# Loading row pairs as 64 KB runs into three slots shared by x and y, in a kernel that takes row-wise cosine similarities

## The chip, the cores and the metric

The kernel runs on one core of one Trainium2 chip. The time is device microseconds (us) of one execution. "Last data" below is the end of the last load packet in the trace's packet records, and "tail" is what follows it until the span ends. A DMA engine is called dry, or idle, when it has no packet under way, and its next packet after that is a restart.

## The reference

```python
x, y: float32 [8192, 8192]
out = sum(x * y, axis=1) / (norm(x, axis=1) * norm(y, axis=1) + 1e-8)
```

Every element of x and y is read once: 536.87 MB. Per row there are three sums: of x*x, y*y and x*y.

## The kernel before

A tile is 128 rows, one row of 32 KB on each partition. x and y have two buffers each. VectorE takes the dot (product and sum in one instruction); ScalarE takes the two sums of squares. SyncE issues the loads of tile t+2 as soon as tile t is free.

```python
xpool = tile_pool(name="xpool", bufs=2); ypool = tile_pool(name="ypool", bufs=2)
...
def issue_dma(t):                       # last tile: cut into 2 and 5 pieces
    nc.sync.dma_start(out=xtiles[t], in_=xv[t])      # 128 runs of 32 KB
    nc.sync.dma_start(out=ytiles[t], in_=yv[t])
...
def compute_tile(t):
    nc.vector.tensor_tensor_reduce(out=prod_s, in0=xt, in1=yt, ..., accum_out=xy_acc[:, t:t+1])  # prod_s bf16
    nc.scalar.activation(out=sq_s, in_=xt, func=Square, accum_out=xx_acc[:, t:t+1])
    nc.scalar.activation(out=sq_s, in_=yt, func=Square, accum_out=yy_acc[:, t:t+1])
...
# last tile: VectorE also squares the first 2048 columns of x, ScalarE the rest
```

Of the kernel before, what the change touches and what calls it, by code (L numbers as in the profile page):

```python
# [7 lines left out]


@with_exitstack  # L10
def kernel(
# [6 lines left out]
    nc = tc.nc  # L18
    P = nc.NUM_PARTITIONS

    n_rows, n_cols = x.shape
    assert n_rows % P == 0
    n_tiles = n_rows // P

    fp32 = mybir.dt.float32
    bf16 = mybir.dt.bfloat16

    xv = x.rearrange("(t p) k -> t p k", p=P)
    yv = y.rearrange("(t p) k -> t p k", p=P)

    xpool = ctx.enter_context(tc.tile_pool(name="xpool", bufs=2))
    ypool = ctx.enter_context(tc.tile_pool(name="ypool", bufs=2))
    sqpool = ctx.enter_context(tc.tile_pool(name="sqpool", bufs=1))
    prodpool = ctx.enter_context(tc.tile_pool(name="prodpool", bufs=1))
    accpool = ctx.enter_context(tc.tile_pool(name="accpool", bufs=1))
    finpool = ctx.enter_context(tc.tile_pool(name="finpool", bufs=1))
    psumpool = ctx.enter_context(tc.tile_pool(name="psum", bufs=1, space=bass.MemoryType.PSUM))

    xtiles = [
        xpool.tile([P, n_cols], fp32, tag="x", name=f"xt{t}")  # L40
        for t in range(n_tiles)
    ]
    ytiles = [
        ypool.tile([P, n_cols], fp32, tag="y", name=f"yt{t}")
        for t in range(n_tiles)
    ]

    last = n_tiles - 1

    HALF = n_cols // 2  # L50

    XCH = [(0, HALF), (HALF, n_cols)]
    Q = n_cols // 8
    YCH = [(0, 2 * Q), (2 * Q, 4 * Q), (4 * Q, 6 * Q), (6 * Q, 7 * Q), (7 * Q, n_cols)]

    def issue_dma(t):
        if t == last:
            for a, b in XCH:
                nc.sync.dma_start(out=xtiles[t][:, a:b], in_=xv[t, :, a:b])  # L59
            for a, b in YCH:  # L60
                nc.sync.dma_start(out=ytiles[t][:, a:b], in_=yv[t, :, a:b])  # L61
        else:
            nc.sync.dma_start(out=xtiles[t], in_=xv[t])  # L63
            nc.sync.dma_start(out=ytiles[t], in_=yv[t])  # L64

    issue_dma(0)
    issue_dma(1)

    dummy = finpool.tile([P, 1], fp32, tag="dummy")
    nc.scalar.memzero(dummy)  # L70
    nc.scalar.sqrt(out=dummy, in_=dummy)  # L71

    ident = finpool.tile([P, P], fp32, tag="ident")
    make_identity(nc, ident)

    xx_acc = accpool.tile([P, n_tiles], fp32, tag="xx")
    yy_acc = accpool.tile([P, n_tiles], fp32, tag="yy")
    xy_acc = accpool.tile([P, n_tiles], fp32, tag="xy")

    prod_s = prodpool.tile([P, n_cols], bf16, tag="prod")  # L80
    sq_s = sqpool.tile([P, n_cols], bf16, tag="sq")

    res = finpool.tile([P, n_tiles], fp32, tag="res")
    nn = finpool.tile([P, n_tiles], fp32, tag="nn")
    den = finpool.tile([P, n_tiles], fp32, tag="den")
    rcp = finpool.tile([P, n_tiles], fp32, tag="rcp")
    res_t_ps = psumpool.tile([n_tiles, P], fp32, tag="res_t_ps")
    res_t = finpool.tile([n_tiles, P], fp32, tag="res_t")
    res_t_ps_last = psumpool.tile([2, P], fp32, tag="res_t_ps_last")
    res_row_last = finpool.tile([2, P], fp32, tag="res_row_last")  # L90
    out_v = out.rearrange("(t p) -> t p", p=P)

    def compute_tile(t):
        xt = xtiles[t]
        yt = ytiles[t]
        nc.vector.tensor_tensor_reduce(  # L96
            out=prod_s,
            in0=xt,
            in1=yt,
            scale=1.0,  # L100
            scalar=0.0,
            op0=mybir.AluOpType.mult,
            op1=mybir.AluOpType.add,
            accum_out=xy_acc[:, t:t + 1],
        )
        nc.scalar.activation(  # L106
            out=sq_s,
            in_=xt,
            func=mybir.ActivationFunctionType.Square,
            accum_out=xx_acc[:, t:t + 1],  # L110
        )
        nc.scalar.activation(  # L112
            out=sq_s,
            in_=yt,
            func=mybir.ActivationFunctionType.Square,
            accum_out=yy_acc[:, t:t + 1],
        )

    def chain(cols, ps, sb, orows):
        nc.vector.tensor_tensor(  # L120
            out=nn[:, cols], in0=xx_acc[:, cols], in1=yy_acc[:, cols],
            op=mybir.AluOpType.mult,
        )
        nc.scalar.activation(  # L124
            out=den[:, cols], in_=nn[:, cols],
            func=mybir.ActivationFunctionType.Sqrt,
        )
        nc.vector.reciprocal(out=rcp[:, cols], in_=den[:, cols])  # L128
        nc.vector.tensor_tensor(  # L129
            out=res[:, cols], in0=xy_acc[:, cols], in1=rcp[:, cols],  # L130
            op=mybir.AluOpType.mult,
        )
        nc.tensor.transpose(out=ps, in_=res[:, cols], identity=ident)  # L133
        nc.vector.tensor_copy(out=sb, in_=ps)  # L134
        nc.sync.dma_start(out=out_v[orows, :], in_=sb)

    for t in range(n_tiles - 1):
        if t + 2 < n_tiles:
            issue_dma(t + 2)
# [114 lines left out]
```

## Time and profile before

| | before |
|---|---|
| time, median | 1256.36 us (1256.19 to 1256.38, 3 runs) |
| span of the profiled run | 1254.4 us |
| bytes read, mean rate | 536.87 MB, 428 GB/s |
| ScalarE busy, VectorE busy | 73%, 45% |
| last data, tail | 1248.1 us, 6.3 us |

The page's rows of 40 equal slices show how busy the DMA engines are (9 is 90% or more) and what they moved. All but the last slice are full. A packet is counted whole in the slice in which it starts, so the GB/s row scatters.

```profile
DMA  9999999999999999999999999999999999999997
GB/s 401 435 435 435 429 430 428 435 434 435 429 429 430 434 433 435 429 428 432 434 434 435 428 428 432 435 434 434 428 428 433 435 433 433 427 430 432 435 434 307
DMA packets 19227, 536.97 MB, mean 428 GB/s; under 512 B 2132, under 2 KB 2196, under 8 KB 2452
```

The Trainium skill, "DMA: Bandwidth & Descriptors", section "Where 436 GB/s comes from", gives a ceiling of 435.2 GB/s on the side of the core's on-chip memory. The best slices here show 435; with each packet spread over its length, the slices between the first and the last lie at 431 to 433. So the trace agrees within 1%. At that rate the bytes need 1233.6 us (an estimate: 536.87 MB over 435.2 GB/s).

The chain that ended last, by engine, says the same: three quarters of it is waiting for loads.

```profile
DMA 76%; DVE 22%; SPq 1%; issue 1%; DVEq 0%; PE 0%; ACT 0%
```

The costliest groups (columns: line, engine, operation, tiles, shapes, count | busy us, mean ns of one | idle us before them and what ended it) give the durations: 8.69 us for a dot over 8192 columns, 7.03 us for a square.

```profile
L96 DVE CUSTOM_DVE_ANT_0 prod_s<-xt,yt 128x8192 bf16<-128x8192 f32 x63 | 547.6, 8692 | 687.5 <-DMA yt<-in_y_dram 687.5
L106 ACT ACTIVATE sq_s<-xt 128x8192 bf16<-128x8192 f32 x63 | 442.9, 7031 | 168.5 <-DMA xt<-in_x_dram 168.5
```

The timeline of one tile (columns: start us, length us, engine, line, operation; the idle time before it and its releaser in brackets) shows the rhythm.

```profile
606.17 7.03 ACT L112 ACTIVATE sq_s<-yt 128x8192 bf16<-128x8192 f32 x1 [2.59 <-DMA yt<-in_y_dram]
606.25 8.69 DVE L96 CUSTOM_DVE_ANT_0 prod_s<-xt,yt 128x8192 bf16<-128x8192 f32 x1 [10.72 <-DMA yt<-in_y_dram]
...
615.01 0.33 SPq L63 DMA_DIRECT2D xt<-in_x_dram  x1
615.43 0.38 SPq L64 DMA_DIRECT2D yt<-in_y_dram  x1
...
626.01 8.69 DVE L96 CUSTOM_DVE_ANT_0 prod_s<-xt,yt 128x8192 bf16<-128x8192 f32 x1 [11.06 <-DMA yt<-in_y_dram]
```

y lands, the dot runs from 606.25, and 8.76 us later SyncE issues the next x and y. At that moment x of the next tile is about to land and its y, which lands at 626.0, is queued behind it, so the DMA engines still have about 11 us of work. What the issue waits for is the dot.

The issues (last column: us from issue to landing) show that loads wait in a queue: 9.7 us of transfer (8 packets of 1.21 us on each DMA engine) takes 20 to 30 us from issue to landing.

```profile
xt<-in_x_dram SPq DMA_DIRECT2D x63, 4096.0 KB, 20.2
yt<-in_y_dram SPq DMA_DIRECT2D x63, 4096.0 KB, 29.5
```

### The profile page before, as it was taken

The numbers are of one execution on the slowest core, as the hardware profiler recorded it, in microseconds if no ns is written. First come the engines' busy times: TensorE is split into PE (matmuls) and PEld (weight loads), VectorE is DVE, ScalarE is ACT, GpSimd is POOL, SyncE is SP. The second block draws the span as 40 slices with busy tenths as digits, with TensorE's granted clock in tenths as the row PEclk, the third lists the DMA queues.
The fourth block names the chain that finished last, engine by engine and source line by source line (L and its number), as shares of the span: only waits on it lengthen the run. The fifth ranks groups of instructions, "written<-read, shape, count | busy, mean of one in ns | idle before, by whom it ended". The sixth has DMA issues, their size and how long they took to land.

```text
span 1254.4 us, 933 instructions
## 1 busy us (share of the span) xinstructions
PE 0.8 (0%) x2; PEld 0.2 (0%) x2; DVE 561.6 (45%) x147; ACT 915.0 (73%) x276; POOL 0.7 (0%) x6
## 2 busy tenths in 40 slices
PE   0000000000000000000000000000000000000000
PEld 0000000000000000000000000000000000000000
DVE  2354353443534535445354353453544525445356
ACT  5777767776777767776777767776777767776777
POOL 0000000000000000000000000000000000000000
DMA  9999999999999999999999999999999999999997
GB/s 401 435 435 435 429 430 428 435 434 435 429 429 430 434 433 435 429 428 432 434 434 435 428 428 432 435 434 434 428 428 433 435 433 433 427 430 432 435 434 307
DMA packets 19227, 536.97 MB, mean 428 GB/s; under 512 B 2132, under 2 KB 2196, under 8 KB 2452
## 3 DMA queue, kind: packets, MB, share of 16 engines
q1 hardware_dynamic: 19220, 536.91, 99.5%
q14 instruction: 7, 0.06, 0.0%
HBM read 536.87 MB, written 0.03 MB: 428 GB/s over the span
## 4 chain that ended last, share of the span: by engine, by line
DMA 76%; DVE 22%; SPq 1%; issue 1%; DVEq 0%; PE 0%; ACT 0%
DMA yt<-in_y_dram 76%; DVE prod_s L96 21%; SPq L63 1%; DVE prod_s L186 0%; DVEq L96 0%; SPq L64 0%; SPq L61 0%; SPq L59 0%; DVE xy_acc L96 0%; PE res_t_ps_last L221 0%; DVE res_row_last L222 0%; ACT den L212 0%; DVE rcp L216 0%; DVE res L217 0%; DVE xy_acc L204 0%
## 5 line engine op out<-in xcount | busy, mean ns | idle before, releaser
L96 DVE CUSTOM_DVE_ANT_0 prod_s<-xt,yt 128x8192 bf16<-128x8192 f32 x63 | 547.6, 8692 | 687.5 <-DMA yt<-in_y_dram 687.5
L106 ACT ACTIVATE sq_s<-xt 128x8192 bf16<-128x8192 f32 x63 | 442.9, 7031 | 168.5 <-DMA xt<-in_x_dram 168.5
L112 ACT ACTIVATE sq_s<-yt 128x8192 bf16<-128x8192 f32 x63 | 443.0, 7031 | 164.2 <-DMA yt<-in_y_dram 164.2
L112 ACT ACTIVATION_READ_ACCUMULATOR sq_s<-yt 128x1 f32 x63 | 11.8, 188 | 0.0
L106 ACT ACTIVATION_READ_ACCUMULATOR sq_s<-xt 128x1 f32 x63 | 11.8, 187 | 0.0
L186 DVE CUSTOM_DVE_ANT_0 prod_s<-xt,yt 128x2048 bf16<-128x2048 f32 (+1 forms) x5 | 9.2, 1864 | 1.6 <-DMA yt<-in_y_dram 1.5
L180 ACT ACTIVATE sq_s<-yt 128x2048 bf16<-128x2048 f32 (+1 forms) x5 | 7.8, 1551 | 0.0
L96 DVE DVE_READ_ACCUMULATOR2_ANT xy_acc<- 128x1 f32 x63 | 5.2, 83 | 0.0
L173 ACT ACTIVATE sq_s<-xt 128x4096 bf16<-128x4096 f32 x1 | 3.6, 3617 | 0.6 <-DMA xt<-in_x_dram 0.6
L157 DVE CUSTOM_DVE_ANT_0 prod_s<-xt 128x2048 bf16<-128x2048 f32 x1 | 2.3, 2291 | 0.0
L167 ACT ACTIVATE sq_s<-xt 128x2048 bf16<-128x2048 f32 x1 | 1.9, 1911 | 0.0
L70 ACT ACT_TABLE_LOAD x1 | 1.3, 1283 | 0.7 <-PEq L238 0.7
L124 ACT ACTIVATE den<-nn 128x62 f32<-128x62 f32 x1 | 0.3, 257 | 1.8 <-DVE nn L120 1.8
L71 ACT ACT_TABLE_LOAD x1 | 1.3, 1283 | 0.0
L133 PE MATMUL res_t_ps<-ident,res 128*62 128x128 f32 x1 | 0.4, 392 | 1219.7 <-DVE res L129 1219.7
L180 ACT ACTIVATION_READ_ACCUMULATOR sq_s<-yt 128x1 f32 x5 | 0.9, 186 | 0.0
L128 DVE RECIPROCAL rcp<-den 128x62 f32<-128x62 f32 x1 | 0.5, 541 | 0.3 <-ACT den L124 0.3
L134 DVE COPY res_t<-res_t_ps 62x128 f32<-62x128 f32 x1 | 0.3, 282 | 0.6 <-PE res_t_ps L133 0.6
L212 ACT ACTIVATE den<-nn 128x2 f32<-128x2 f32 x1 | 0.2, 204 | 0.4 <-DVE nn L208 0.4
L222 DVE COPY res_row_last<-res_t_ps_last 2x128 f32<-2x128 f32 x1 | 0.3, 278 | 0.5 <-PE res_t_ps_last L221 0.5
L186 DVE DVE_READ_ACCUMULATOR2_ANT xyp<- 128x1 f32 x5 | 0.4, 83 | 0.0
L221 PE MATMUL res_t_ps_last<-ident,res 128*2 128x128 f32 x1 | 0.4, 371 | 31.6 <-DVE res L217 31.6
(23 smaller groups left out, 3.8 us busy)
## 6 DMA issues: line engine op xcount, KB each, us to landing
xt<-in_x_dram SPq DMA_DIRECT2D x63, 4096.0 KB, 20.2
yt<-in_y_dram SPq DMA_DIRECT2D x63, 4096.0 KB, 29.5
xt<-in_x_dram SPq DMA_DIRECT2D x2, 2048.0 KB, 19.9
yt<-in_y_dram SPq DMA_DIRECT2D x3, 1024.0 KB, 24.0
yt<-in_y_dram SPq DMA_DIRECT2D x2, 512.0 KB, 27.1
out_dram<-res_t SPq DMA_DIRECT2D x1, 31.0 KB
out_dram<-res_row_last SPq DMA_DIRECT2D x1, 1.0 KB
```

Of the source, the lines that this page charges most:

```text
L63: nc.sync.dma_start(out=xtiles[t], in_=xv[t])
L70: nc.scalar.memzero(dummy)
L71: nc.scalar.sqrt(out=dummy, in_=dummy)
L96: nc.vector.tensor_tensor_reduce(out=prod_s, in0=xt, in1=yt, scale=1.0, scalar=0.0, op0=mybir.AluOpType.mult, op1=mybir.AluOpType.add, acc ...
L106: nc.scalar.activation(out=sq_s, in_=xt, func=mybir.ActivationFunctionType.Square, accum_out=xx_acc[:, t:t + 1],)
L112: nc.scalar.activation(out=sq_s, in_=yt, func=mybir.ActivationFunctionType.Square, accum_out=yy_acc[:, t:t + 1],)
L128: nc.vector.reciprocal(out=rcp[:, cols], in_=den[:, cols])
L157: nc.vector.tensor_tensor_reduce(out=prod_s[:, 0:SPL], in0=xt[:, 0:SPL], in1=xt[:, 0:SPL], scale=1.0, scalar=0.0, op0=mybir.AluOpType.mult ...
L167: nc.scalar.activation(out=sq_s[:, SPL:HALF], in_=xt[:, SPL:HALF], func=mybir.ActivationFunctionType.Square, accum_out=xxp[:, 1:2],)
L173: nc.scalar.activation(out=sq_s[:, HALF:], in_=xt[:, HALF:], func=mybir.ActivationFunctionType.Square, accum_out=xxp[:, 2:3],)
L180: nc.scalar.activation(out=sq_s[:, a:b], in_=yt[:, a:b], func=mybir.ActivationFunctionType.Square, accum_out=yyp[:, k:k + 1],)
L186: nc.vector.tensor_tensor_reduce(out=prod_s[:, a:b], in0=xt[:, a:b], in1=yt[:, a:b], scale=1.0, scalar=0.0, op0=mybir.AluOpType.mult, op1= ...
```

## The change

The intent: two adjacent rows of HBM are one contiguous run of 64 KB, so the number of runs and of loads halves. Two such buffers for x and two for y would need 256 KB on each partition; with three, 192 KB, the memory is already full. So three slots of 64 KB rotate through x and y together. The next y goes into the slot of the current x, which therefore has to be freed while the current y is still in use. To free it sooner, the last 896 columns of x are copied aside first and their products are taken last. To save memory, products overwrite x (float32 instead of a bf16 scratch), and squares go to a uint8 scratch. The tail keeps its five y pieces but gives all of the last x to ScalarE.

```diff
-    xpool = ...bufs=2;  ypool = ...bufs=2;  sq_s, prod_s: bf16 [P, 8192]
+    SIDE = 896
+    xg = x[0:G*2*P, :].rearrange("(g p j) k -> g p (j k)", p=P, j=2)   # yg alike; G = 31
+    slots = ...tile_pool(name="slots", bufs=3)        # [P, 2*K] float32 each
+    junk = [P, K] uint8;  side = [P, SIDE] float32
+    def load(g):
+        xs[g] = slot(f"xg{g}"); nc.sync.dma_start(out=xs[g], in_=xg[g])
+        ys[g] = slot(f"yg{g}"); nc.sync.dma_start(out=ys[g], in_=yg[g])
...
+    def dot(a, b, acc, init=0.0):                     # products written over a
+        nc.vector.tensor_tensor_reduce(out=a, in0=a, in1=b, ..., scalar=init, accum_out=acc)
+    for g in range(G):
+        square(xt[:, 0:K], ...); square(xt[:, K:], ...)
+        nc.vector.tensor_copy(out=side, in_=xt[:, 2*K - SIDE:])
+        dot(xt[:, 0:K], yt[:, 0:K], xy[:, c:c+1])
+        dot(xt[:, K:2*K - SIDE], yt[:, K:2*K - SIDE], xyh[:, c+1:c+2])      # frees x's slot
+        square(yt[:, 0:K], ...); square(yt[:, K:], ...)
+        dot(side, yt[:, 2*K - SIDE:], xy[:, c+1:c+2], init=xyh[:, c+1:c+2]) # frees y's slot
+        if g + 1 < G: load(g + 1)
...                                                   # last two tiles: plain 32 KB rows in two slots
-    VectorE squares columns 0:2048 of the last x
+    square(s1[:, 0:H], ...); square(s1[:, H:K], ...)  # all on ScalarE
```

More of the change, by code (lines that the diff above doesn't have):

```diff
@@ L7 @@
 from concourse._compat import with_exitstack
+FP32 = mybir.dt.float32
+U8 = mybir.dt.uint8
+ALU = mybir.AluOpType
+ACTF = mybir.ActivationFunctionType
+EPS = 1e-8
 @with_exitstack
@@ L19 @@
     P = nc.NUM_PARTITIONS
-    n_rows, n_cols = x.shape
-    assert n_rows % P == 0
-    n_tiles = n_rows // P
-    fp32 = mybir.dt.float32
-    bf16 = mybir.dt.bfloat16
+    n_rows, K = x.shape
+    G = n_rows // (2 * P) - 1
+    SIDE = 896
+    xg = x[0:G * 2 * P, :].rearrange("(g p j) k -> g p (j k)", p=P, j=2)
+    yg = y[0:G * 2 * P, :].rearrange("(g p j) k -> g p (j k)", p=P, j=2)
     xv = x.rearrange("(t p) k -> t p k", p=P)
     yv = y.rearrange("(t p) k -> t p k", p=P)
-    xpool = ctx.enter_context(tc.tile_pool(name="xpool", bufs=2))
@@ L32 @@
-    ypool = ctx.enter_context(tc.tile_pool(name="ypool", bufs=2))
-    sqpool = ctx.enter_context(tc.tile_pool(name="sqpool", bufs=1))
-    prodpool = ctx.enter_context(tc.tile_pool(name="prodpool", bufs=1))
-    accpool = ctx.enter_context(tc.tile_pool(name="accpool", bufs=1))
-    finpool = ctx.enter_context(tc.tile_pool(name="finpool", bufs=1))
-    psumpool = ctx.enter_context(tc.tile_pool(name="psum", bufs=1, space=bass.MemoryType.PSUM))
-    xtiles = [
-        xpool.tile([P, n_cols], fp32, tag="x", name=f"xt{t}")
-        for t in range(n_tiles)
-    ]
@@ L43 @@
-    ytiles = [
-        ypool.tile([P, n_cols], fp32, tag="y", name=f"yt{t}")
-        for t in range(n_tiles)
-    ]
-    last = n_tiles - 1
-    HALF = n_cols // 2
-    XCH = [(0, HALF), (HALF, n_cols)]
-    Q = n_cols // 8
-    YCH = [(0, 2 * Q), (2 * Q, 4 * Q), (4 * Q, 6 * Q), (6 * Q, 7 * Q), (7 * Q, n_cols)]
-    def issue_dma(t):
-        if t == last:
-            for a, b in XCH:
-                nc.sync.dma_start(out=xtiles[t][:, a:b], in_=xv[t, :, a:b])
-            for a, b in YCH:
-                nc.sync.dma_start(out=ytiles[t][:, a:b], in_=yv[t, :, a:b])
-        else:
-            nc.sync.dma_start(out=xtiles[t], in_=xv[t])
-            nc.sync.dma_start(out=ytiles[t], in_=yv[t])
@@ L66, with slot @@
-    issue_dma(0)
-    issue_dma(1)
-    dummy = finpool.tile([P, 1], fp32, tag="dummy")
+    nt = n_rows // P
+    slots = ctx.enter_context(tc.tile_pool(name="slots", bufs=3))
+    sidepool = ctx.enter_context(tc.tile_pool(name="side", bufs=1))
+    small = ctx.enter_context(tc.tile_pool(name="small", bufs=1))
+    psumpool = ctx.enter_context(
+        tc.tile_pool(name="psum", bufs=1, space=bass.MemoryType.PSUM))
+    def slot(name):
+        return slots.tile([P, 2 * K], FP32, tag="slot", name=name)
@@ new lines @@
+    xs, ys = {}, {}
+    def load(g):
+        xs[g] = slot(f"xg{g}")
+        nc.sync.dma_start(out=xs[g], in_=xg[g])
+        ys[g] = slot(f"yg{g}")
+        nc.sync.dma_start(out=ys[g], in_=yg[g])
+    load(0)
+    xx = small.tile([P, nt], FP32, tag="xx")
+    yy = small.tile([P, nt], FP32, tag="yy")
+    xy = small.tile([P, nt], FP32, tag="xy")
+    xyh = small.tile([P, nt], FP32, tag="xyh")
+    den = small.tile([P, nt], FP32, tag="den")
+    rcp = small.tile([P, nt], FP32, tag="rcp")
+    res = small.tile([P, nt], FP32, tag="res")
@@ L70 @@
+    ident = small.tile([P, P], FP32, tag="ident")
+    dummy = small.tile([P, 1], FP32, tag="dummy")
+    junk = sidepool.tile([P, K], U8, tag="junk")
+    side = sidepool.tile([P, SIDE], FP32, tag="side")
     nc.scalar.memzero(dummy)
     nc.scalar.sqrt(out=dummy, in_=dummy)
-    ident = finpool.tile([P, P], fp32, tag="ident")
     make_identity(nc, ident)
-    xx_acc = accpool.tile([P, n_tiles], fp32, tag="xx")
-    yy_acc = accpool.tile([P, n_tiles], fp32, tag="yy")
-    xy_acc = accpool.tile([P, n_tiles], fp32, tag="xy")
@@ L80 @@
-    prod_s = prodpool.tile([P, n_cols], bf16, tag="prod")
-    sq_s = sqpool.tile([P, n_cols], bf16, tag="sq")
-    res = finpool.tile([P, n_tiles], fp32, tag="res")
-    nn = finpool.tile([P, n_tiles], fp32, tag="nn")
-    den = finpool.tile([P, n_tiles], fp32, tag="den")
-    rcp = finpool.tile([P, n_tiles], fp32, tag="rcp")
-    res_t_ps = psumpool.tile([n_tiles, P], fp32, tag="res_t_ps")
-    res_t = finpool.tile([n_tiles, P], fp32, tag="res_t")
-    res_t_ps_last = psumpool.tile([2, P], fp32, tag="res_t_ps_last")
@@ L90 @@
-    res_row_last = finpool.tile([2, P], fp32, tag="res_row_last")
-    out_v = out.rearrange("(t p) -> t p", p=P)
-    def compute_tile(t):
-        xt = xtiles[t]
-        yt = ytiles[t]
-        nc.vector.tensor_tensor_reduce(
-            out=prod_s,
-            in0=xt,
-            in1=yt,
-            scale=1.0,
-            scalar=0.0,
-            op0=mybir.AluOpType.mult,
-            op1=mybir.AluOpType.add,
-            accum_out=xy_acc[:, t:t + 1],
-        )
-        nc.scalar.activation(
-            out=sq_s,
-            in_=xt,
-            func=mybir.ActivationFunctionType.Square,
-            accum_out=xx_acc[:, t:t + 1],
-        )
-        nc.scalar.activation(
-            out=sq_s,
-            in_=yt,
-            func=mybir.ActivationFunctionType.Square,
-            accum_out=yy_acc[:, t:t + 1],
-        )
@@ L119, in chain @@
-    def chain(cols, ps, sb, orows):
-        nc.vector.tensor_tensor(
-            out=nn[:, cols], in0=xx_acc[:, cols], in1=yy_acc[:, cols],
-            op=mybir.AluOpType.mult,
-        )
-        nc.scalar.activation(
-            out=den[:, cols], in_=nn[:, cols],
-            func=mybir.ActivationFunctionType.Sqrt,
-        )
-        nc.vector.reciprocal(out=rcp[:, cols], in_=den[:, cols])
-        nc.vector.tensor_tensor(
-            out=res[:, cols], in0=xy_acc[:, cols], in1=rcp[:, cols],
-            op=mybir.AluOpType.mult,
-        )
-        nc.tensor.transpose(out=ps, in_=res[:, cols], identity=ident)
-        nc.vector.tensor_copy(out=sb, in_=ps)
-        nc.sync.dma_start(out=out_v[orows, :], in_=sb)
@@ L137 @@
-    for t in range(n_tiles - 1):
-        if t + 2 < n_tiles:
-            issue_dma(t + 2)
-        compute_tile(t)
-        if t == n_tiles - 3:
-            e = slice(0, last - 1)
-            chain(e, res_t_ps[e, :], res_t[e, :], e)
-    lcol = slice(last, last + 1)
-    tcols = slice(last - 1, last + 1)
-    xt = xtiles[last]
-    yt = ytiles[last]
-    SPL = 2048
-    xxp = accpool.tile([P, 3], fp32, tag="xxp")
-    nych = len(YCH)
-    yyp = accpool.tile([P, nych], fp32, tag="yyp")
-    xyp = accpool.tile([P, nych], fp32, tag="xyp")
@@ L154 @@
-    xx_fold_s = accpool.tile([P, 3], fp32, tag="xxfolds")
-    yy_fold_s = accpool.tile([P, nych], fp32, tag="yyfolds")
-    nc.vector.tensor_tensor_reduce(
-        out=prod_s[:, 0:SPL],
-        in0=xt[:, 0:SPL],
-        in1=xt[:, 0:SPL],
-        scale=1.0,
-        scalar=0.0,
-        op0=mybir.AluOpType.mult,
-        op1=mybir.AluOpType.add,
-        accum_out=xxp[:, 0:1],
-    )
-    nc.scalar.activation(
-        out=sq_s[:, SPL:HALF],
-        in_=xt[:, SPL:HALF],
-        func=mybir.ActivationFunctionType.Square,
-        accum_out=xxp[:, 1:2],
-    )
@@ L173 @@
-    nc.scalar.activation(
-        out=sq_s[:, HALF:],
-        in_=xt[:, HALF:],
-        func=mybir.ActivationFunctionType.Square,
-        accum_out=xxp[:, 2:3],
-    )
-    for k, (a, b) in enumerate(YCH):
-        nc.scalar.activation(
-            out=sq_s[:, a:b],
-            in_=yt[:, a:b],
-            func=mybir.ActivationFunctionType.Square,
-            accum_out=yyp[:, k:k + 1],
-        )
-        nc.vector.tensor_tensor_reduce(
-            out=prod_s[:, a:b],
-            in0=xt[:, a:b],
-            in1=yt[:, a:b],
-            scale=1.0,
-            scalar=0.0,
-            op0=mybir.AluOpType.mult,
-            op1=mybir.AluOpType.add,
-            accum_out=xyp[:, k:k + 1],
-        )
@@ L196 @@
-    nc.scalar.activation(
-        out=xx_fold_s, in_=xxp, func=mybir.ActivationFunctionType.Copy,
-        accum_out=xx_acc[:, lcol],
-    )
-    nc.scalar.activation(
-        out=yy_fold_s, in_=yyp, func=mybir.ActivationFunctionType.Copy,
-        accum_out=yy_acc[:, lcol],
-    )
-    nc.vector.tensor_reduce(
-        out=xy_acc[:, lcol], in_=xyp, axis=mybir.AxisListType.X,
-        op=mybir.AluOpType.add,
-    )
-    nc.vector.tensor_tensor(
-        out=nn[:, tcols], in0=xx_acc[:, tcols], in1=yy_acc[:, tcols],
-        op=mybir.AluOpType.mult,
-    )
@@ L212 @@
-    nc.scalar.activation(
-        out=den[:, tcols], in_=nn[:, tcols],
-        func=mybir.ActivationFunctionType.Sqrt,
-    )
-    nc.vector.reciprocal(out=rcp[:, tcols], in_=den[:, tcols])
-    nc.vector.tensor_tensor(
-        out=res[:, tcols], in0=xy_acc[:, tcols], in1=rcp[:, tcols],
-        op=mybir.AluOpType.mult,
-    )
-    nc.tensor.transpose(out=res_t_ps_last[0:2, :], in_=res[:, tcols], identity=ident)
-    nc.vector.tensor_copy(out=res_row_last[0:2, :], in_=res_t_ps_last[0:2, :])
@@ L223, with square @@
-    nc.sync.dma_start(out=out_v[last - 1:last + 1, :], in_=res_row_last[0:2, :])
+    def square(src, acc):
+        nc.scalar.activation(
+            out=junk[:, 0:src.shape[-1]], in_=src, func=ACTF.Square,
+            accum_out=acc)
+    def dot(a, b, acc, init=0.0):
+        nc.vector.tensor_tensor_reduce(
+            out=a, in0=a, in1=b, scale=1.0,
+            scalar=init, op0=ALU.mult, op1=ALU.add, accum_out=acc)
+    for g in range(G):
+        xt, yt = xs.pop(g), ys.pop(g)
+        c = 2 * g
+        square(xt[:, 0:K], xx[:, c:c + 1])
+        square(xt[:, K:], xx[:, c + 1:c + 2])
+        nc.vector.tensor_copy(out=side, in_=xt[:, 2 * K - SIDE:])
+        dot(xt[:, 0:K], yt[:, 0:K], xy[:, c:c + 1])
+        dot(xt[:, K:2 * K - SIDE], yt[:, K:2 * K - SIDE], xyh[:, c + 1:c + 2])
+        square(yt[:, 0:K], yy[:, c:c + 1])
+        square(yt[:, K:], yy[:, c + 1:c + 2])
+        dot(side, yt[:, 2 * K - SIDE:], xy[:, c + 1:c + 2], init=xyh[:, c + 1:c + 2])
+        if g + 1 < G:
+            load(g + 1)
@@ new lines, in finish @@
+    def finish(cols):
+        nc.vector.tensor_mul(out=den[:, cols], in0=xx[:, cols], in1=yy[:, cols])
+        nc.scalar.activation(out=den[:, cols], in_=den[:, cols], func=ACTF.Sqrt)
+        nc.vector.tensor_scalar_add(out=den[:, cols], in0=den[:, cols], scalar1=EPS)
+        nc.vector.reciprocal(out=rcp[:, cols], in_=den[:, cols])
+        nc.vector.tensor_mul(out=res[:, cols], in0=xy[:, cols], in1=rcp[:, cols])
+    s0 = slot("tail0")
+    s1 = slot("tail1")
+    nc.sync.dma_start(out=s0[:, 0:K], in_=xv[nt - 2])
@@ new lines @@
+    nc.sync.dma_start(out=s0[:, K:], in_=yv[nt - 2])
+    H = K // 2
+    Q = K // 8
+    XCH = [(0, H), (H, K)]
+    YCH = [(0, 2 * Q), (2 * Q, 4 * Q), (4 * Q, 6 * Q), (6 * Q, 7 * Q), (7 * Q, K)]
+    for a, b in XCH:
+        nc.sync.dma_start(out=s1[:, a:b], in_=xv[nt - 1, :, a:b])
+    for a, b in YCH:
+        nc.sync.dma_start(out=s1[:, K + a:K + b], in_=yv[nt - 1, :, a:b])
+    gcols = slice(0, 2 * G)
+    finish(gcols)
+    orow = small.tile([G, P, 2], FP32, tag="orow")
+    for j in range(2):
+        ps = psumpool.tile([G, P], FP32, tag=f"ps{j}", name=f"ps{j}")
+        nc.tensor.transpose(out=ps, in_=res[:, j:2 * G:2], identity=ident)
+        nc.vector.tensor_copy(out=orow[:, :, j], in_=ps)
@@ new lines @@
+    nc.sync.dma_start(
+        out=out[0:G * 2 * P].rearrange("(g q) -> g q", q=2 * P),
+        in_=orow.rearrange("g p j -> g (p j)"))
+    c = nt - 2
+    square(s0[:, 0:K], xx[:, c:c + 1])
+    square(s0[:, K:], yy[:, c:c + 1])
+    dot(s0[:, 0:K], s0[:, K:], xy[:, c:c + 1])
+    c = nt - 1
+    xxp = small.tile([P, 2], FP32, tag="xxp")
+    yyp = small.tile([P, len(YCH)], FP32, tag="yyp")
+    xyp = small.tile([P, len(YCH)], FP32, tag="xyp")
+    fold = small.tile([P, len(YCH)], FP32, tag="fold")
@@ new lines @@
+    square(s1[:, 0:H], xxp[:, 0:1])
+    square(s1[:, H:K], xxp[:, 1:2])
+    for k, (a, b) in enumerate(YCH):
+        square(s1[:, K + a:K + b], yyp[:, k:k + 1])
+        dot(s1[:, a:b], s1[:, K + a:K + b], xyp[:, k:k + 1])
+    nc.scalar.activation(out=fold[:, 0:2], in_=xxp, func=ACTF.Copy, accum_out=xx[:, c:c + 1])
+    nc.scalar.activation(out=fold, in_=yyp, func=ACTF.Copy, accum_out=yy[:, c:c + 1])
+    nc.vector.tensor_reduce(
+        out=xy[:, c:c + 1], in_=xyp, axis=mybir.AxisListType.X, op=ALU.add)
@@ L227 @@
+    tcols = slice(nt - 2, nt)
+    finish(tcols)
+    psl = psumpool.tile([2, P], FP32, tag="psl")
+    orl = small.tile([2, P], FP32, tag="orl")
+    nc.tensor.transpose(out=psl, in_=res[:, tcols], identity=ident)
+    nc.vector.tensor_copy(out=orl, in_=psl)
+    nc.sync.dma_start(out=out.rearrange("(t p) -> t p", p=P)[nt - 2:nt, :], in_=orl)
 _INS = ['x', 'y']
```

## The prediction

> **What bounds the kernel now: the load stream.** 536.87 MB are read. The row of slices shows DMA at 90% or more in all but the last of 40 slices, at 428 to 435 GB/s. The Trainium skill, "DMA: Bandwidth & Descriptors", section "Where 436 GB/s comes from", puts the ceiling at 435.2 GB/s; this trace agrees (best slices 435). At that rate the bytes alone take 1233.6 us (estimate). ScalarE is 73% busy, VectorE 45%. A tile pair arrives every 19.45 us (timeline: starts of VectorE's dots), against 14.3 us for two squares (7.03 + 0.19 us each) and 8.7 us for one dot. The chain of waits is 76% DMA.
>
> **What the change does to the stream.** In the packet records a 32 KB packet starts every 1209 to 1218 ns on one DMA engine, where the bytes need 1205 ns; each load adds a 6 ns semaphore write.  64 KB runs halve the packets and the loads. Estimate: 38.91 us per 16.8 MB now, 38.64 to 38.77 after, so 4 to 8 us off over 32 such groups, centre 6. If 64 KB runs are cut back into 32 KB packets, the gain is under 1 us.
>
> **Does the three-slot rotation starve the stream?** When y of group g lands, only x of g+1 is queued (19.3 us of work). The load of y g+1 waits for two dots: 0.62 us from last packet to VectorE start (trace) + 8.70 + 7.75 us (estimate for 7296 columns from 8.69 for 8192) + 0.1 = 17.2 us. From issue to first packet took 1.03 to 1.74 us at the kernel's start. So packets are ready at 18.2 to 18.9 us, 0.4 to 1.1 us before the slowest DMA engine runs dry. Engines drift apart by 0.5 us early and 2.3 us late in the trace, so the leading ones will run dry, but that alone costs nothing; a cold restart (first packets 1.6 to 2.1 us instead of 1.2) can make one the last. I add 1.5 us in total. Float32 products over x and uint8 squares I expect to cost nothing; the side copy (under 1 us) hides in VectorE's idle time.
>
> **The tail gets worse.** Now the last data packet ends at 1248.15 us and the span at 1254.4: 6.3 us. The new tail gives all of the last x to ScalarE (VectorE took 2048 columns before), and ScalarE is blocked behind the Sqrt of the first 62 columns, which waits for the last dot of group 30. Counted from the landing of y30: Sqrt done at 18.7, two squares of tile 62 to 33.0, the x halves to 40.4, the five y pieces to 48.5, folds, Sqrt, transpose, store to about 52.7, while the last data land at 38.7. So 14 us after the last data, 7.7 us more than now. Dots overwrite x that ScalarE must square first; this delays VectorE, but ScalarE stays last.
>
> **Sum:** 1256.4 - 6 + 1.5 + 7.7 = 1259.6, call it 1259 us, range 1252 to 1268. Chances: faster 0.02, same 0.91, slower 0.07.
>
> **What the profile would show.** Packets about 9,900 instead of 19,227 and every middle slice at 431 GB/s or more: step 1 right. y's issue-to-landing near 21 to 22 us, x's near 40; no slice under 420: step 2 right. ScalarE without waits for DMA over the last 30 us, 14 us between last landing and end: step 3 right.
>
> **What would make it wrong:** 64 KB packets that run slower than two of 32 KB; a real bubble in each group (1 us each would be 31 us, slower); an in-place float32 dot slower than 8.7 us; more packets.

## More of the kernel before

The waits of SyncE's queue (waited for: us in total, times, longest):

```profile
SPq L63 <- DVE xy_acc L96: 1144.1, 61, 28.9
```

## The result

| | before | changed |
|---|---|---|
| time, median | 1256.34 us (4 runs) | 1286.17 us (1283.66 to 1288.25, 4 runs) |
| span of the profiled run | 1254.4 us | 1281.5 us |
| mean rate | 428 GB/s | 419 GB/s |
| time for 16.8 MB (one group) | 38.91 us | 39.69 us (38.69 to 40.95) |
| last data, tail | 1248.1 us, 6.3 us | 1273.0 us, 8.6 us |

The ratio is 1.0237, with a 95% interval of 1.0222 to 1.0252: slower by more than 2%. A ratio is the mean time of one kernel's fast runs over that of the other's of the same rounds, so it is not quite the ratio of the medians quoted. The profiled run is the fastest of the four (1283.66 us). The time of one group is the spacing of the first dots of successive groups in the timeline (before: of every second tile).

The slices of the changed kernel: DMA still looks busy, but the rate swings between 395 and 450 GB/s. Part of that swing is the way of counting (450 is above the ceiling): with each 64 KB packet spread over its length, the slices between the first and the last lie at 408 to 434 GB/s, against 431 to 433 before. The sag is real, the peaks are not. The packets have nearly halved, so the 64 KB runs are real.

```profile
DMA  9999999999999999999999999999999999999996
GB/s 425 421 425 430 419 407 444 430 395 444 407 423 425 428 425 419 413 421 415 425 425 425 425 422 422 401 426 425 425 450 415 407 428 428 423 423 421 428 420 275
DMA packets 10266, 536.96 MB, mean 419 GB/s; under 512 B 1139, under 2 KB 1172, under 8 KB 1428
```

The chain that ended last now has less waiting for loads, and 38% dots.

```profile
DMA 57%; DVE 38%; ACT 2%; issue 2%; DVEq 0%; SPq 0%; PE 0%; ACTq 0%
```

The groups show that the dots and squares themselves cost what they did. The dot's mean of 8223 ns mixes 8192 columns with 7296; the two forms take 8.69 and 7.75 us in the timeline below. The uint8 squares take the same 7.03 us. So float32 products over x cost nothing.

```profile
L82 DVE CUSTOM_DVE_ANT_0 xg<-xg,yg 128x8192 f32<-128x8192 f32 (+1 forms) x62 | 507.5, 8223 | 608.0 <-DMA yg<-in_y_dram 608.0
...
L76 ACT ACTIVATE junk<-xg 128x8192 uint8<-128x8192 f32 x62 | 435.9, 7030 | 174.9 <-DMA xg<-in_x_dram 173.9
```

The timeline of a group that took 38.75 us:

```profile
599.87 8.69 DVE L82 CUSTOM_DVE_ANT_0 xg<-xg,yg 128x8192 f32<-128x8192 f32 x1 [20.80 <-DMA yg<-in_y_dram]
...
608.49 7.75 DVE L82 CUSTOM_DVE_ANT_0 xg<-xg,yg 128x7296 f32<-128x7296 f32 x1
...
616.28 0.33 SPq L55 DMA_DIRECT2D yg<-in_y_dram  x1
616.29 1.15 DVE L82 CUSTOM_DVE_ANT_0 side<-side,yg,xyh 128x896 f32<-128x896 f32 x1
...
617.51 0.33 SPq L53 DMA_DIRECT2D xg<-in_x_dram  x1
619.21 7.03 ACT L76 ACTIVATE junk<-xg 128x8192 uint8<-128x8192 f32 x1 [5.11 <-DMA xg<-in_x_dram]
...
638.62 8.69 DVE L82 CUSTOM_DVE_ANT_0 xg<-xg,yg 128x8192 f32<-128x8192 f32 x1 [18.77 <-DMA yg<-in_y_dram]
```

y lands at 599.4. Two dots run. SyncE issues the next y (line 55) at 616.28; the next x (line 53) follows 1.2 us later. The last packet of the x that is already on its way ends at 618.8 (ScalarE starts on it at 619.21). So when y's load is issued, 2.4 us of queued work are left, against about 11 us in the kernel before. The queue's waits show what it waits for: the dot, in all 30 groups.

```profile
SPq L55 <- DVE xyh L82: 1101.5, 30, 38.0
```

The issues: y lands 23.1 us after its issue, of which 19.3 us are transfer.

```profile
xg<-in_x_dram SPq DMA_DIRECT2D x31, 41.4
yg<-in_y_dram SPq DMA_DIRECT2D x31, 23.1
```

The tail (first dot of the last group, last square, last store): the store is issued 46.7 us after the last group's y was ready.

```profile
1232.87 8.69 DVE L82 CUSTOM_DVE_ANT_0 xg<-xg,yg 128x8192 f32<-128x8192 f32 x1 [19.10 <-DMA yg<-in_y_dram]
...
1276.24 1.06 ACT L76 ACTIVATE junk<-tail 128x1024 uint8<-128x1024 f32 x1
...
1279.52 0.26 SPq L158 DMA_DIRECT2D out_dram<-orl  x1
```

Where the time came from: last data is 24.8 us later (1273.0 against 1248.1), and the tail is 2.3 us longer. Together that is the 27.1 us between the spans. Thirty groups at 39.69 instead of 38.91 us make 23.4 us of it.

**Inside one load.** The profile records every packet with its start and length. I sorted the 64 KB packets by the DMA engine that must have carried them (the engine is not recorded; packets that follow one another without a gap are put on one engine; about 40 of 7,936 fit badly, so counts are good to a few per cent). A packet on an engine that was not idle takes 2.42 us. Over the 30 loads of y, an engine was found idle before its first packet in 239 of 480 cases. Of these restarts 10% came within 0.98 us of the issue, half within 1.33, 90% within 2.91, and the latest after 3.87 us; where an engine had been dry, the first packet took about 3.1 us instead of 2.42. Two neighbouring groups (their lengths here by the last packet of y), times after the issue of y's load:

```
group 4 to 5 (40.80 us): 14 engines go on without a gap, one pauses for 0.27 us;
                         one starts 3.32 us after the issue, having been idle for 1.14 us, first packet 3.71 us
group 5 to 6 (38.86 us): that one engine is 2.8 us behind the first; the other 15 run dry,
                         14 of them start 0.95 to 1.38 us after the issue, first packets 2.86 to 3.28 us
```

These times are counted from the issue. The late engine of the first group finished its x only 2.18 us after the issue and then idled for 1.14 us. That costs the group 2 us, because a load has landed only when its last engine has. The Trainium skill says the same in "DMA: Bandwidth & Descriptors", section "Why a DMA increments its semaphore by 16 and not by 1": the engines finish independently and only the full count means that all data are there. The second group loses next to nothing.

### The profile page after: what moved, and what is told of

Its sections match the earlier page's. It is cut to its first block, busy times and chain, and to the rows that moved or that the text cites. A ratio compares the mean times of both kernels' runs of the same rounds, so it can differ in the third digit from the quotient of the medians.

```text
span 1281.5 us, 845 instructions
## 1 busy us (share of the span) xinstructions
PE 1.0 (0%) x3; PEld 0.3 (0%) x3; DVE 583.6 (46%) x241; ACT 916.8 (72%) x276; POOL 0.7 (0%) x6
## 4 chain that ended last, share of the span: by engine, by line
DMA 57%; DVE 38%; ACT 2%; issue 2%; DVEq 0%; SPq 0%; PE 0%; ACTq 0%
DMA yg<-in_y_dram 57%; DVE xg L82 38%; ACT junk L76 2%; DVEq L82 0%; DVE xyh L82 0%; SPq L53 0%; PE psl L156 0%; ACT den L102 0%; ACT fold L149 0%; DVE orl L157 0%; DVE xy L82 0%; DVE den L103 0%; DVE rcp L104 0%; DVE den L101 0%; DVE res L105 0%
## 5 line engine op out<-in xcount | busy, mean ns | idle before, releaser
L82 DVE CUSTOM_DVE_ANT_0 xg<-xg,yg 128x8192 f32<-128x8192 f32 (+1 forms) x62 | 507.5, 8223 | 608.0 <-DMA yg<-in_y_dram 608.0
L76 ACT ACTIVATE junk<-yg 128x8192 uint8<-128x8192 f32 x62 | 435.9, 7030 | 185.2 <-DMA yg<-in_y_dram 184.3
L76 ACT ACTIVATE junk<-xg 128x8192 uint8<-128x8192 f32 x62 | 435.9, 7030 | 174.9 <-DMA xg<-in_x_dram 173.9
L91 DVE COPY side<-xg 128x896 f32<-128x896 f32 x31 | 19.4, 627 | 78.1 <-DMA xg<-in_x_dram 78.1
L82 DVE CUSTOM_DVE_ANT_0 side<-side,yg,xyh 128x896 f32<-128x896 f32 x31 | 35.7, 1152 | 1.1
L76 ACT ACTIVATE junk<-tail 128x2048 uint8<-128x2048 f32 (+3 forms) x9 | 29.1, 3234 | 0.2
L82 DVE CUSTOM_DVE_ANT_0 tail<-tail 128x2048 f32<-128x2048 f32 (+2 forms) x6 | 17.8, 2998 | 1.1 <-DMA tail<-in_y_dram 1.1
L76 ACT ACTIVATION_READ_ACCUMULATOR junk<-yg 128x1 f32 x62 | 11.6, 186 | 0.0
L76 ACT ACTIVATION_READ_ACCUMULATOR junk<-xg 128x1 f32 x62 | 11.6, 186 | 0.0
L82 DVE DVE_READ_ACCUMULATOR2_ANT xy<- 128x1 f32 x63 | 5.2, 83 | 0.0
## 6 DMA issues: line engine op xcount, KB each, us to landing
yg<-in_y_dram SPq DMA_DIRECT2D x31, 23.1
```

The lines of the kernel that those rows point to most:

```text
L76: nc.scalar.activation(out=junk[:, 0:src.shape[-1]], in_=src, func=ACTF.Square, accum_out=acc)
L82: nc.vector.tensor_tensor_reduce(out=a, in0=a, in1=b, scale=1.0, scalar=init, op0=ALU.mult, op1=ALU.add, accum_out=acc)
L91: nc.vector.tensor_copy(out=side, in_=xt[:, 2 * K - SIDE:])
```

## The experiments

Two theories at the start. **A, starvation:** the y load is issued so late that DMA engines run dry, and a restart takes longer than the work left in the queue. **B, slow runs:** 64 KB runs or paired rows are slow in themselves, for HBM or for the DMA engines. All runs below gave correct results. "y issue" is the time from y's last packet to the issue of the next y load; in the changed kernel it is 16.9 us, and 19.3 us is when the queue is empty.

### e1: a shorter side

```diff
-    SIDE = 896
+    SIDE = 128
```

> Only SIDE is changed, 896 to 128, so the load of y for the next group is issued 0.8 us later (17.7 us after y lands instead of 16.9), with 1.6 us of queued work left instead of 2.4. Theory A (the queue runs dry at each y load, restart of a DMA engine takes 1 to 4 us): the mean group period rises from 39.7 us to 40 to 40.8, the time from 1286 to 1295 to 1320 us. Rival B (64 KB runs or paired rows are slow in themselves, wherever the load is issued): 1286 us, no change.

Measured: 1304.33 us (1303.50 to 1306.47), ratio 1.0384; group 40.39 us on average. As theory A said, and not B: the same packets became slower only because a load was issued 0.8 us later.

### e2: control for e3

```diff
-    junk = sidepool.tile([P, K], U8)
+    junk = psumpool.tile([P, 2048], FP32)
-    square(xt[:, 0:K], xx[:, c:c+1])                # and the others
+    for i in range(4): square(xt[:, i*2048:(i+1)*2048], xx4[:, 4*c+i:4*c+i+1])
```

> Control for the next run: squares in four pieces of 2048, written as float32 to PSUM, SIDE still 896. Both theories: the stream as in the changed kernel, group period 39.4 to 40, last data near 1274 us; ScalarE's tail 2 to 4 us longer; 1284 to 1292 us.

Measured: 1291.95 us (1290.42 to 1293.27), ratio 1.0283; group 39.83 us; last data 1277.9 us; tail 12.7 us. The stream is that of the changed kernel, as expected. The tail is longer by 4.1 us, a little over the 2 to 4 expected.

### e3: a longer side in the memory that e2 freed

```diff
-    SIDE = 896      # of e2
+    SIDE = 2432
```

> As the control, but the SBUF that the squares gave up goes to SIDE = 2432: y's load issued 1.6 us earlier (15.3 us after y lands), 4.0 us of queued work left. 64 KB runs and pairing unchanged. Theory A: most restarts disappear, group period 38.7 to 39.0, last data 1243 to 1255 us, time 1254 to 1268 us. Rival B: as the control, 1284 to 1292 us.

Measured: 1264.82 us (1264.25 to 1265.25), ratio 1.0067. The y issue is at 15.4 us, 1.6 us earlier than in e2. The group takes 38.90 us, the last data come at 1247.8 us, 30 us earlier than in e2, and the tail is 14.6 us. Only 23 restarts from idle are left. Its slices, which have the same 64 KB packets as the changed kernel, no longer sag in the middle (419 is now the lowest of those between the first and the last two, against 395; spread by length, 423 against 408):

```profile
GB/s 415 440 436 434 422 438 436 432 428 428 432 432 434 426 434 434 430 426 434 428 434 434 438 436 432 428 430 430 434 430 436 428 419 426 432 432 432 432 417 215
```

This decides between A and B: 1.6 us of earlier issue is worth 27 us.

### e4: y in two loads, one for each row of the slot

Three fixed tiles replace the rotating pool, so that half a slot can be loaded as soon as that half is free.

```diff
-    nc.sync.dma_start(out=ys[g], in_=yg[g])
+    for a, b in ((0, K), (K, 2*K)):
+        nc.sync.dma_start(out=ys[g][:, a:b], in_=yg[g][:, a:b])
```

> Only the y load is cut, into two of 4 MB with 32 KB runs; the first needs only the first row of x's slot, free after the first dot, so it is issued 9.3 us after y lands, with 10 us of queued work left. x keeps 64 KB runs. Theory A: no engine runs dry, group period 38.7 to 38.9, last data 1243 to 1250 us, ScalarE-bound tail, time 1250 to 1260 us. Rival B (64 KB runs slow in themselves): only half of the loads are cured, time about 1270 us.

Measured: 1255.78 us (1255.75 to 1255.93), ratio 0.9996 (0.9979 to 1.0012); group 38.83 us, most of them 38.78; last data 1246.8 us; tail 7.2 us. The timeline shows the dot of the first row starting when the first half of y has landed. The first half of the next y is issued when that dot is done (the two issues of y are merged into one line of 9.11 us):

```profile
1158.77 8.69 DVE L87 CUSTOM_DVE_ANT_0 slot<-slot,slot 128x8192 f32<-128x8192 f32 x1 [9.12 <-DMA slot<-in_y_dram]
...
1167.50 9.11 SPq L60 DMA_DIRECT2D slot<-in_y_dram  x2
```

The current y ends 0.4 us after that issue and the next x at 1187.2, so 19.7 us of queued work are left, and not the 10 us expected. The whole loss is gone at no cost in memory, with x still in 64 KB runs. Rival B's 1270 us is excluded, though y is in 32 KB runs again here; e3 and e10, in which all groups have 64 KB runs, are the cleaner answer to B.

### e5: the next x load later (failed as a test)

The start of y could be late because the next x load is issued 1.2 us behind it. That is rival C.

```diff
+    for _ in range(6): nc.vector.tensor_copy(out=side, in_=side)
     dot(side, yt[:, 2*K - SIDE:], ...)
```

> Six in-place copies of side (about 0.6 us each) between the dot that releases x's slot and the last dot. The y load is issued as in the changed kernel; only the x load that follows it comes 3.7 us later (5 us after y's instead of 1.2), which is still over 16 us before it is needed. Theory A (a restart is slow by itself): period 39.4 to 40.0, time 1279 to 1292 us. Rival C (the x load issued 1.2 us after y's load holds up y's start on some engines): the late restarts vanish, period 38.7 to 39.1, time 1255 to 1268 us.

Measured: 1285.07 us (1280.40 to 1291.43), group 39.96 us. The copies depend on nothing but side, and the timeline shows that the scheduler put them into VectorE's idle time before the dots, and x's load was still issued 1.2 us after y's. The run only repeats the changed kernel. e13 is the test that this was meant to be.

### e6: 32 KB runs, everything else as changed

```diff
-    x[...].rearrange("(g p j) k -> g p (j k)", p=P, j=2)
+    x[...].rearrange("(g j p) k -> g p j k", p=P, j=2)      # rows 128 apart: two runs of 32 KB
```

> Rotation, SIDE and issue order as in the changed kernel, but each 8.4 MB load takes two rows that are 128 rows apart, so its runs are 32 KB again. Theory A: the starvation stays, time 1280 to 1298 us (the same loss, plus up to 8 us for twice as many packets). Rival B (64 KB runs or paired rows are slow): back to 1252 to 1262 us.

Measured: 1296.49 us (1293.77 to 1300.79), ratio 1.0323; group 40.26 us. The loss stays without the 64 KB runs, and is somewhat larger. So the pairing of rows, the headline of the change, is not what made it slow.

### e7: a bf16 side of 4864 columns

```diff
-    SIDE = 2432;  side: float32      # of e3
+    SIDE = 4864;  side: bf16
```

> As e3, with side in bf16 so that 4864 columns fit: the y load is issued about 12.8 us after y lands, 6.5 us of queued work left, above every restart seen so far (at most 4.6 us after the issue). 64 KB runs kept. Theory A: no engine runs dry, every group 38.63 to 38.75 us, last data 1239 to 1244 us, ScalarE tail of about 14.5 us as in e3, time 1254 to 1261 us. Rival B: no better than e3 (1265 us).

Measured: 1263.86 us (1263.23 to 1264.48), ratio 1.0060. The y issue is at 12.9 us and 8 restarts are left, but the last data come at 1247.3 us: the expected 1239 to 1244 us is a miss. Most groups take 38.71 us, yet seven take 39.33 to 39.40. In each of those seven the packet records have an 8 KB packet on the queue that the profile names "instruction" (taken here for the fetch of instructions), and one 64 KB packet that takes 2.80 instead of 2.42 us. Three more such fetches fall into groups of 38.70 to 38.77 us, so a fetch does not always lengthen a group. Squares in four pieces had quadrupled ScalarE's instructions.

### e8: e7 with a new tail

```diff
+    jt = slot("jtail")     # third slot: scratch for squares and products of the last two tiles
+    VectorE: squares of columns 0:2048 of the last x but one, of 0:4096 of the last x
```

> e7 with a new tail: VectorE squares 2048 columns of the last x but one and half of the last x, tail squares and products go to the third slot in whole pieces, so no dot waits for a square. Theory A: last data 1239 to 1244 us as in e7, tail 8 to 10 us, time 1249 to 1255 us, faster than before by 0.1 to 0.6%.

Measured: 1259.60 us (1259.35 to 1259.91), ratio 1.0026; last data 1247.1 us; tail 10.9 us. The tail is 3.2 us shorter than in e7, less than hoped, and the stream is e7's. A miss.

### e9: all engines dry (failed as a test)

Two theories of why a restart is late: only while other engines stream (D), or at random (E).

```diff
+    for _ in range(10): nc.vector.tensor_copy(out=side, in_=side)
     dot(xt[:, K:2*K - SIDE], yt[:, K:2*K - SIDE], ...)
```

> Ten in-place copies of side before the releasing dot: the y load is issued 5.8 us later, 22.7 us after y lands, when all 16 DMA engines have been dry for over 2 us and none is moving data. Theory D (a restart is slow only while other engines stream): all engines start 0.9 to 1.7 us after the issue as at the kernel's start, first packets about 3.1 us, group periods nearly equal (44.0 to 44.6 us, spread under 0.5), time 1415 to 1432 us. Rival E (a restart is late at random, whatever the others do): starts up to 4 us after the issue, periods spread over 2 us as in the changed kernel, mean 44.7 to 46.5 us, time over 1432 us.

Measured: 1283.94 us (2 runs), the changed kernel once more. The timeline shows why: the copies ran after the dots and beside the next x, and y was issued when it always was.

```profile
605.28 7.75 DVE L82 CUSTOM_DVE_ANT_0 xg<-xg,yg 128x7296 f32<-128x7296 f32 x1
...
613.07 0.33 SPq L55 DMA_DIRECT2D yg<-in_y_dram  x1
...
616.75 6.58 DVE L94 COPY side<-side 128x896 f32<-128x896 f32 x10
```

### e10: fewer instructions

```diff
-    four squares of 2048 into PSUM;  SIDE = 4864     # of e7
+    two squares of 4096 into uint8;  SIDE = 3328     # bf16
```

> Between the changed kernel and e7: squares in two pieces of 4096 instead of four of 2048 (half the added ScalarE instructions), bf16 side of 3328 columns, y load issued about 14.4 us after y lands (4.9 us of work left). In e7 seven groups were 0.69 us longer, each at an 8 KB instruction fetch on the instruction queue. If those fetches are the cause: 3 or 4 such groups, mean period 38.75 to 38.82, last data 1243 to 1246.5 us, time 1256 to 1262 us. If they are not: seven again, as e7, mean period 38.86.

Measured: 1258.01 us (1257.25 to 1258.21), ratio 1.0011; group 38.77 us on average, 38.71 for most, three over 39 us; last data 1244.7 us. All as expected if the fetches are the cause. The page counts them (queue, kind: packets, MB, share), first e7, then e10:

```profile
q14 instruction: 12, 0.10, 0.0%
```

```profile
q14 instruction: 8, 0.07, 0.0%
```

Before and changed have 7 and 6. Of the seven fetches of e10 before its last group, three fall into the three long groups, three into groups that are 0.1 to 0.2 us long, and one into a group of the usual length. The link is one of time and of count; no run removes the fetches alone.

### e11: e4 with a shorter tail

```diff
+    VectorE squares columns 0:2048 of the last x;  y in seven pieces instead of five
```

> e4 with a shorter tail: VectorE squares 2048 columns of the last x as in the kernel before, and the last y comes in seven pieces instead of five. Stream as e4 (last data near 1247 us), tail 5.5 to 6.5 us instead of 7.2, time 1254 to 1255.4 us, ratio to before 0.998 to 0.9995.

Measured: 1257.00 us (1256.73 to 1257.08), ratio 1.0004. A miss: the tail grew from 7.2 to 8.1 us. The timeline shows the load of a late piece being issued only at 1232.7, and ScalarE ending the squares of the small pieces last. The run changed two things at once, so which of them cost the 0.9 us is not shown.

### e12: e10 with e8's tail

```diff
+    e8's tail; VectorE squares 1024 columns of the last x but one
```

> e10 (64 KB runs, y load issued early enough) with e8's tail, VectorE squaring 1024 columns of the last x but one and half of the last x. Stream as e10: last data near 1244.7 us. Tail 7 to 9 us instead of 10.7 (the new tail took 3.2 us off in e8). Time 1253.5 to 1256 us, ratio to before 0.9975 to 0.9995.

Measured: 1255.51 us (1255.42 to 1255.70), ratio 0.9993 (0.9979 to 1.0007); last data 1244.8 us; tail 8.9 us. As expected, but not clear of the kernel before.

### e13: the next x load later, done right

The copy writes y's slot, so it must follow the dots that read it, and x's load must wait for it.

```diff
+    nc.vector.tensor_copy(out=yt[:, K:2*K - SIDE], in_=yt[:, K:2*K - SIDE])
     dot(side, yt[:, 2*K - SIDE:], ...)
```

> What e5 was to be: an in-place copy of 7296 columns of y (about 5 us), which the scheduler cannot hoist because it must follow the releasing dot, before the last dot. y's load is issued as in the changed kernel, the next x load over 5 us after it instead of 1.2. Theory A (the y load's own restart is slow): period 39.3 to 40.1, time 1278 to 1292 us. Rival C (the x load that follows 1.2 us later holds up y's start): starts all under 2 us after the issue, period 38.7 to 39.1, time 1255 to 1268 us.

Measured: 1284.30 us (1283.38 to 1287.17), ratio 1.0226; group 39.70 us. The y load is issued at 613.54, the x load now 5.2 us behind it:

```profile
613.54 0.33 SPq L55 DMA_DIRECT2D yg<-in_y_dram  x1
613.62 3.96 DVE L96 COPY yg<-yg 128x7296 f32<-128x7296 f32 x1
...
618.71 0.33 SPq L53 DMA_DIRECT2D xg<-in_x_dram  x1
```

Restarts are as late as ever (226 of them, 90% below 3.04 us, the latest 4.26 us after the issue). Rival C falls.

### e14: all engines dry, done right

```diff
+    nc.vector.tensor_copy(out=xt[:, 0:K], in_=xt[:, 0:K])
     dot(xt[:, K:2*K - SIDE], yt[:, K:2*K - SIDE], ...)
```

> What e9 was to be: an in-place copy of x's first 8192 columns (about 5.7 us) between the dots and the release of x's slot, so the y load is issued about 22.6 us after y lands, when all 16 DMA engines are dry. Theory D (a restart is late only while other engines stream): all start 0.9 to 1.7 us after the issue, group periods 43.8 to 44.6 us with a spread under 0.5, time 1408 to 1432 us. Rival E (late at random): starts up to 4 us after the issue, periods spread over 2 us, mean over 44.7, time over 1432 us.

Measured: 1376.67 us (2 runs), ratio 1.0957. The time expected was too long because the copy took 4.42 us and not 5.7, so y was issued 21.3 us after it landed and not 22.6; the periods, which are what the test is about, behave as theory D says. They run from 42.57 to 43.03 us, a spread of 0.46 us, against 2.26 us in the changed kernel.

```profile
597.79 8.69 DVE L82 CUSTOM_DVE_ANT_0 xg<-xg,yg 128x8192 f32<-128x8192 f32 x1 [20.33 <-DMA yg<-in_y_dram]
...
614.09 0.08 DVE L82 DVE_READ_ACCUMULATOR2_ANT xyh<- 128x1 f32 x1
614.09 4.42 DVE L93 COPY xg<-xg 128x8192 f32<-128x8192 f32 x1
...
618.57 0.33 SPq L55 DMA_DIRECT2D yg<-in_y_dram  x1
...
640.36 8.69 DVE L82 CUSTOM_DVE_ANT_0 xg<-xg,yg 128x8192 f32<-128x8192 f32 x1 [20.12 <-DMA yg<-in_y_dram]
```

All 480 restarts come from idle engines, and they start 0.97 to 1.54 us after the issue (10% and 90%; the latest 2.08, and 24 of them later than the 1.7 us that theory D allowed), with first packets of 3.1 us. In the changed kernel the latest came after 3.87 us. So with all engines dry the late restarts are gone, and rival E, lateness at random whatever the state of the engines, falls.

Theory D is not shown by this, because e14 leaves a rival standing that was not named. All 16 engines were dry when y was issued, so what makes a restart late may be that the other engines stream (D), or that the late engine itself still had work at the issue (call it F). The packet records of the changed kernel fit both. In 27 of its 30 groups all 16 engines had a packet under way at the issue, and 17 of these groups have a restart later than 2.41 us. In the other three groups 10 to 13 engines were already dry at the issue, and every restart came by 2.40 us. No run was built to keep one engine dry at the issue while the others stream on. What in the chip makes the difference stays open.

### e15: e12 with its tail taken apart

```diff
+    the first 60 columns are finished before group 30 (group 30: two plain tiles, 32 KB runs)
+    squares of the last x but one into the uint8 scratch, which is free at once
```

> e12 with its tail untangled: the results of the first 60 columns are finished before group 30 (group 30 is loaded as two plain tiles with 32 KB runs), so no Sqrt waits for the last dot of group 30 in ScalarE's queue, and the squares of the last x but one use the uint8 scratch that is free at once. Stream as e12 (last data near 1245 us), tail 6 to 7.5 us instead of 8.9, time 1253 to 1254.6 us, ratio to before 0.9970 to 0.9988.

Measured: 1253.71 us (1253.48 to 1253.82), ratio 0.9980 (0.9966 to 0.9993); last data 1245.0 us; tail 6.8 us. This one beats the kernel before by 0.2%, which the interval supports but which is less than the 2% that would count as faster here, and the changed kernel by 2.5% (the two medians, from different rounds). The page's rate and packets:

```profile
GB/s 406 431 436 436 436 436 436 436 434 436 436 434 436 436 425 431 425 431 436 436 436 434 436 436 434 436 436 436 431 427 423 430 436 434 436 434 436 420 434 293
DMA packets 10542, 536.98 MB, mean 429 GB/s; under 512 B 1155, under 2 KB 1189, under 8 KB 1445
```

### The runs in one view

Only runs that set the issue time apart are listed; the others stand in their own sections. "Issue" is y's issue after y's landing, "group" the mean time of a group, both in us.

| run | issue | group | spread of groups | last data | tail | time |
|---|---|---|---|---|---|---|
| before | - | 38.91 | 38.77 to 39.54 | 1248.1 | 6.3 | 1256.3 |
| e14, all dry | 21.3 | 42.75 | 42.57 to 43.03 | 1367.6 | 6.9 | 1376.7 |
| e1, side 128 | 17.7 | 40.39 | 39.11 to 41.84 | 1295.7 | 6.9 | 1304.3 |
| changed, side 896 | 16.9 | 39.69 | 38.69 to 40.95 | 1273.0 | 8.6 | 1286.2 |
| e3, side 2432 | 15.4 | 38.90 | 38.68 to 39.50 | 1247.8 | 14.6 | 1264.8 |
| e10, side 3328 bf16 | 14.5 | 38.77 | 38.60 to 39.38 | 1244.7 | 10.7 | 1258.0 |
| e7, side 4864 bf16 | 12.9 | 38.86 | 38.62 to 39.40 | 1247.3 | 14.1 | 1263.9 |
| e15, as e10, tail mended | 14.5 | 38.78 | 38.62 to 39.39 | 1245.0 | 6.8 | 1253.7 |

## Why the prediction was wrong

- **"What bounds the kernel now": right.** Where the stream was fed in time, the time followed the stream and the tail (e4, e10, e15).
- **The gain of 64 KB runs: right in kind, a little smaller in size.** Packets fell to 10,266. With the stream fed, a group without a fetch takes 38.71 us (e7, e10) against 38.86 for the usual pair of tiles before: 0.15 us, or 4.8 us over 32 such groups. e4, with half of its bytes in 64 KB runs, lies between (38.78). The prediction had 4 to 8 us, centre 6.
- **"Engines ... will run dry, but that alone costs nothing; ... I add 1.5 us in total": this is the step that failed.** The issue time was right (17.2 us predicted, 16.9 measured), and so was the warning that a bubble of 1 us per group would cost 31 us. The term that was mis-sized is the restart. I took it from the kernel's start, 1.03 to 1.74 us from issue to first packet, when nothing else moves and every engine is idle. That is the restart of e14 (0.97 to 1.54 us), and with it the changed kernel would indeed lose nothing: 16.9 + 1.5 + 0.7 + 19.3 = 38.4 us, less than 38.7 (an estimate from these measured parts). But in the changed kernel most engines still move x when y is issued, and a restart then comes up to 3.9 us after the issue: 16.9 + 3.3 + 1.3 + 19.3 = 40.8 us for the group shown above. Thirty groups lost 1.0 us each (39.69 against 38.71), 29 us, where 1.5 us had been put down. "That alone costs nothing" had assumed that an engine that runs dry has its next packet 1.03 to 1.74 us after the issue whatever it was doing before. Why it does not is open (D or F, see e14).
- **A second error in the same step:** running dry is not confined to the leading engines. In groups 4 to 8 one late engine falls 2 to 3 us behind; in the next group 13 to 15 engines run dry, restart together and promptly and are level again; and then the next late restart follows. Long and short groups alternate there (40.80, 38.86, 40.16, 38.81, 40.45 us between the last packets of y). Elsewhere in the trace they do not (40.64, 40.75, 38.74, 38.79 between first dots).
- **The tail: direction right, size wrong.** 14 us predicted, 8.6 measured. ScalarE did work through without waiting for a load, and the span ended 49.2 us after the last packet of group 30's y instead of 52.7, because the scheduler placed the Sqrt behind a square instead of letting it block ScalarE. The last data came 40.6 us after that packet instead of 38.7, which shortened the tail further. The error happened to be in the other direction from the large one.
- **Float32 products, uint8 squares, side copy: right.** 8.69 and 7.03 us as before; the side copy of 0.63 us sits in idle time.
- **The sum:** 1259 us with a range to 1268, against 1286. The range was too narrow for a term that the text itself named as the thing that would break it.

## What to carry to other kernels

When a load waits for a buffer, compare the work left in the queue at its issue with the slowest restart of an engine that still had work at the issue, not with the start of an idle chip: here 2.4 us left was not enough, 4 us nearly was, and 5 us was. A buffer that is loaded and freed in halves (e4) left 19.7 us of queued work at the issue instead of 2.4, without a byte of memory, where larger units took the lead away. A filler that is to delay something must write what the delayed thing waits for, or the scheduler will move it, and the timeline has to be read before the run is believed.

## What the Trainium skill lacked or had wrong

- "DMA: Bandwidth & Descriptors", section "Latency and other measured facts": it gives about 600 ns to the first byte for loads issued by SyncE. With all engines dry that agrees (e14: 0.97 us from the start of an issue instruction of 0.33 us, so 0.64 us after its end, for the fastest tenth). It does not say that an engine that runs dry in a stream can start much later: 0.97 to 3.04 us after the issue (10% and 90%), up to 4.26, in e13. The same section says that HBM latency rises from 0.2 us to 2 us at high load; that would fit, but no run here shows that it is the cause.
- The same page has nothing on the first packet of an engine that had run dry: 3.1 us for 64 KB against 2.42 us on an engine that had not.
- The same page, section "Where 436 GB/s comes from": one sentence says that for HBM to SBUF the HBM side, about 358 GB/s, binds. On this one core the mean was 428 GB/s and the steady slices 431 to 433, within 1% of the 435.2 of the fabric. Only that sentence misleads: the page's section "Measured (HBM→SBUF, 128 partitions, SWDGE, issued from GpSimd)" has 425 GB/s for 16 MB with the other core of the pair idle, and gives about 358 as the share of each core when both stream.
- The same page, section "Why small descriptors are slow (HBM only)": it gives a fixed cost of about 3 cycles per packet as a matter of small ones. A cost per packet is still to be seen between 32 and 64 KB: 38.86 against 38.71 us per 16.8 MB, with 16 packets fewer on each engine, so about 9 ns per packet (an estimate: 0.15 us over 16, which includes two semaphore writes fewer). Whether it is the cost that the page means is not shown.
- No page has the price of an instruction fetch to a full load stream ("Runtime: NRT & Kernel Launch", section "Instruction fetch mechanics", is where it belongs). An 8 KB packet on the instruction queue came with 0.62 to 0.69 us more in each of seven groups of e7 (39.33 to 39.40 against 38.71), and with at most 0.06 us more in three others.
